# Block-0 products in one pass and other spacing in the order of steps, in a four-layer hybrid kernel

## The chip, the cores and the metric

The kernel runs on one core of a Trainium2 chip. The metric is the device time of one execution in microseconds; all times below are of that one core. TensorE multiplies matrices and writes to PSUM, ScalarE (ACT), VectorE (DVE) and GpSimd (POOL) do the elementwise work, and SyncE (SP) issues the DMAs.

## The reference

The input is 16 learned meta tokens followed by 1024 tokens, 1040 in all, with 1024 features in float32. Four layers follow each other, each as `h = h + branch(rmsnorm(h))`: sliding-window attention (layer 0), an mLSTM (layer 1), HGRN2 (layer 2), and attention again (layer 3). Most of the change lies in the mLSTM, which the text calls the second layer. It walks through blocks of 128 tokens (the first holds only the 16 meta tokens), per head with keys of 128 and values of 256:

```python
qk  = (q @ k.T) * exp(D - m_t)                    # causal weights within the block
num = w_inter * (q @ C) + qk @ v                  # from the state, and from the block
den = w_inter * (q @ n) + qk.sum(-1)
h   = num / maximum(abs(den), exp(-m_t))
C_new = w_old * C + (w_s * k).T @ v               # state for the next block
```

HGRN2 (the third layer) is also a recurrence over blocks: a state S of 128 x 128 per head is decayed, added to by `k.T @ v`, and read by the queries of the next block.

## The kernel before, in words

**Accuracy by parts.** Most products are made of reduced-precision pieces: an operand is split into a high part h and a low part l (`split`: ScalarE copies h at L196, VectorE subtracts to get l at L197), and a product is three matmuls into the same accumulator, h by h, h by l and l by h. Projections are such triples over eight pieces of 128 features (L232 with the weights stationary, L282 with the tokens stationary for values, L327 for output projections, whose results are added to x at L330). Weights come by DMA in halves of 128 x 512 and are split in the same way.

**TensorE's order is written by hand.** Every piece of TensorE work is a step `[cost, function, prefetch]`, with a cost in planned nanoseconds (a column counts 1/2.4 ns). The program runs all steps in one long list. On the other engines the instructions of the steps are put in order by a scheduler, by data, engine and priority; `hi` raises the priority of a step's instructions by a fixed offset. A step with an empty function and a cost is only a distance. `weave(a, b)` merges two lists in proportion to their costs: it takes the next step of `a` as soon as the share of `a` that has been taken isn't above the share of `b`. A part of a projection (6 matmuls of 400, 384 or 256 columns) costs 1000, 960 or 640 and can't be divided. Weights are loaded as far ahead as the steps' costs allow (`LOOKAHEAD`, 12000).

**The second layer (`layer_b`).** For each of 8 heads, `mixer` lists for nine blocks the steps s1 (q by k, a transpose of k, then the weights W and the weighted keys kw on the other engines, each split, and the split of V), s2 (the output: W by V, and from block 1 on qw by the state C), s3 (the state: kw by V; the sum is copied into C at L1063 and split) and s4 (transposes of the result). Their costs are 320, 714, 357 and 214. Between s1 of a block and its s2 stands s1 of the next block. The list without its last three steps is woven with the projections for the next head (in head 0: keys of heads 1 and 2 and values of head 1, a planned 42987 ns). Block 0 has 16 rows: its W, kw and V are filled with zeros on GpSimd and then take the same three matmuls of 128 rows as every other block, in `product`, L998.

**The third layer (`layer_c`).** For each head and region of up to two blocks, the tail is: `tail1` (transposes of the decayed keys, L1378, copied to kT at L1380), a distance `KT_LAG`, `states` (kT by V, L1388, then VectorE makes the new S, L1395), a distance `ATT_LAG`, and `tail2` for each block (attention by V at L1409, S by the queries at L1411). Tails are woven with the next region's levels, and the whole with projections.

**Attention (`layer_a`).** Keys are projected in two tiles, each in three chunks of tokens. `evac` in `qk_proj` takes a chunk out of PSUM on ScalarE: the scaled values at L576 and the squares at L577. Some thousand planned ns later `stat` sums the squares with a matmul, L616, and still later `k_split` makes h and l of the result (L509 to L512). The same `evac` serves the query tiles (t is their number, None for keys). Softmax values Sm are normalized on GpSimd at L741 before their transposes at L756.

Of the kernel before, what the change touches and what calls it, by code (L numbers as in the profile page):

```python
# [32 lines left out]

B_COLS = 96
LOOKAHEAD = 12000.0
REST_LAG, REST_STEPS = 600.0, 10
TAIL_LAG = 600.0
PRIO = 40
ROWS, TMPS, RAWS, YS = 8, 6, 2, 3
XS = 14  # L40
GAP, BURST = 200.0, 1300.0
GATE_LAG, GATE_COLS = 2000.0, 17000.0
KT_LAG, ATT_LAG = 900.0, 600.0
NORM_AT = (4000.0, 0.7), (5000.0, 0.5), (8000.0, 0.5)
Y_LAST, Y_EARLY, Y_AHEAD = 3, 8, 2500.0
T_LAG, V_LAG = 2, 4
# [68 lines left out]
def hybrid_kernel(ctx: ExitStack, tc: tile.TileContext, ins, out, layers=(0, 1, 2, 3)):  # L115
# [13 lines left out]
    def nm(x):  # L129
        ctr[0] += 1  # L130
        return f"{x}{ctr[0]}"
# [63 lines left out]
    def split(src, h, l):  # L195
        s.copy(h, src)  # L196
        v.tensor_tensor(l, src, h.bitcast(F32), op=ALU.subtract)  # L197
# [15 lines left out]
    def proj(src, evac, chunks=CHUNKS, early=None):  # L213
        st = {}

        def pre():
            st["w"] = weights(src, "m")

        groups = []
        for n, (c0, cn) in enumerate(chunks):  # L220
            grp = []
            for part in range(4):
                def fn(n=n, c0=c0, cn=cn, part=part):
                    if part == 0:
                        st[n] = psj()
                    if part == 1 and early is not None:
                        early(n, c0, cn)
                    h, l = st["w"]
                    acc = st[n]
                    for k in (2 * part, 2 * part + 1):  # L230
                        for i, (a, b) in enumerate(((h, uh), (h, ul), (l, uh))):
                            pe.matmul(acc[:, :cn], a[:, k, :], b[:, k, c0 : c0 + cn],  # L232
                                      start=(k == 0 and i == 0), stop=(k == KT - 1 and i == 2))
# [247 lines left out]
    def layer_a(i, j, first, last, fin, scale=None):  # L481
        win, wout = ins["a_win"][j], ins["a_wout"][j]
        chunks = LAST_CHUNKS if last else CHUNKS
        R = {}
# [72 lines left out]
        def qk_proj(src, gcol, work, fsplit, ch, t=None, fetched=False):  # L557
# [79 lines left out]
                d = D_K1 if fetched else D_K0 if scaled else D_K  # L637
                return [(d[0], [(8 if scaled else 4) * cn * MM, stat, None]), (d[1], [0.0, rope, None]), (d[2], turn)]

            return proj(src, evac, ch, early if fetched else None), [finish(n, *c) for n, c in enumerate(ch)]  # L640

        def tile_of(groups, events):

# [16 lines left out]
        V = {}  # L660
# [203 lines left out]
    def layer_b(i, j, fin):  # L864
        win, wout = ins["b_win"][j], ins["b_wout"][j]
        R = {}
# [114 lines left out]
        def mixer(h):  # L981
            W = {}

            def start():
                R["h", h, 0], R["h", h, 1] = row(), row()
                fetch(0)

            def fetch(b):
                c0, cn = blk(b)
                W["rw", b] = z = R["mix"].tile([P, 2, P], F32, tag="rw", name=nm("rw"), bufs=3)  # L990
                sp.dma_start(z[:, :, :cn], R["rows_d"][:, h, c0 : c0 + cn].partition_broadcast(P))

            def parts(z, cols=P, bufs=2):
                return [R["mix"].tile([P, cols], F32R, tag=z + q, name=nm(z + q), bufs=bufs) for q in "hl"]

            def product(acc, a, c, start, stop):
                for i, (x0, x1) in enumerate(((0, 0), (0, 1), (1, 0))):
                    pe.matmul(acc, a[x0], c[x1][:, :258], start=(start and i == 0), stop=(stop and i == 2))  # L998

            def s1(b):  # L1000
                mix, q, k = R["mix"], R["q", h], R["k", h]
                c0, cn = blk(b)
                cs = slice(c0, c0 + cn)
                if b + 1 < NB:
                    fetch(b + 1)
                rb, wb = (W["rw", b][:, z, :cn] for z in range(2))
                W["V", b] = parts("V", 258)
                split(R["v", h, b][:, :258], *(z[:, :258] for z in W["V", b]))
                pq = psum("pm", 2)
                pe.matmul(pq[:cn, :cn], k[:, cs], q[:, cs], start=True, stop=True)  # L1010
# [6 lines left out]
                w = mix.tile([P, P], F32, tag="W", name=nm("W"), bufs=2)  # L1017
                if b == 0:
                    g.memset(w, 0.0)
                v.tensor_tensor(w[:cn, :cn], E[:cn, :cn], pq[:cn, :cn], op=ALU.mult)  # L1020
                W["W", b] = parts("W")
                split(w, *W["W", b])
                if b:
                    qw = mix.tile([P, P], F32, tag="W", name=nm("qw"), bufs=2)
                    v.tensor_tensor(qw, q[:, cs], wb, op=ALU.mult)
                    W["qw", b] = parts("qw")
                    split(qw, *W["qw", b])
                if b < NB - 1:
                    W["kw", b] = kh, kl = parts("kw")
                    if b == 0:  # L1030
                        for z in (kh, kl):
                            g.memset(z.bitcast(F32), 0.0)
                    last = E[:cn, cn - 1 : cn]
                    s.activation(kh[:cn], pq[:cn, 128:256], AF.Identity, scale=last)
                    v.scalar_tensor_tensor(kl[:cn], pq[:cn, 128:256], last, kh[:cn].bitcast(F32),
                                           op0=ALU.mult, op1=ALU.subtract)

            def s2(b):
                mix = R["mix"]
                c0, cn = blk(b)  # L1040
                num = psum("po", 1)
                product(num[:, :258], W["W", b], W["V", b], True, b == 0)
                if b:
                    product(num[:, :258], W["qw", b], W["Cs"], False, True)
                den = small(1)
                s.activation(den[:cn], num[:cn, 256:257], AF.Abs)
                v.tensor_tensor(den[:cn], den[:cn], R["em"][:cn, b, h : h + 1], op=ALU.max)
                v.reciprocal(den[:cn], den[:cn])
                W["hn", b] = hn = mix.tile([P, 256], F32, tag="hn", name=nm("hn"), bufs=2)
                if b == 0:  # L1050
                    g.memset(hn, 0.0)
                s.activation(hn[:cn], num[:cn, :256], AF.Identity, scale=den[:cn])

            def s3(b):
                mix = R["mix"]
                c0, cn = blk(b)
                pc = psa()
                product(pc[:, :258], W["kw", b], W["V", b], True, True)
                if b == 0:
                    W["C"] = mix.tile([P, 258], F32, tag="C", name=nm("C"), bufs=1)  # L1060
                C = W["C"][:, :258]
                if b == 0:
                    v.tensor_copy(C, pc[:, :258])  # L1063
                else:
                    v.scalar_tensor_tensor(C, C, W["rw", b][:, 1, cn - 1 : cn], pc[:, :258], op0=ALU.mult, op1=ALU.add)
                W["Cs"] = parts("C", 258, 1)
                split(C, *(z[:, :258] for z in W["Cs"]))

            def s4(b):
                c0, cn = blk(b)  # L1070
                cs = slice(c0, c0 + cn)
                pt = psum("pt", 1)
                for c in range(2):
                    pe.transpose(pt[:, c * P : c * P + P], W["hn", b][:, c * P : c * P + P], ident)
                for c in range(2):
                    v.tensor_copy(R["h", h, c][:, cs], pt[:, c * P : c * P + cn])

            steps = [[0.0, start, None]]
            for b in range(NB + 2):
# [404 lines left out]
    steps = []  # L1484
# [190 lines left out]
```

## Time and profile before

| | |
|---|---|
| median of 3 runs | 2586.45 us (2584.43 to 2587.59) |
| profiled execution | 2586.18 us |
| its span, first to last instruction | 2584.4 us |
| mean granted TensorE clock | 0.996 |
| busy: TensorE, VectorE, ScalarE, GpSimd | 98%, 79%, 67%, 9% |
| stretches, us: layer 0, layer 1, hand-over, layer 2, layer 3 | 0 to 476, to 1460, to 1540, to 2095, to the end (about) |

Matmuls are pipelined, so a matmul's own duration is longer than its distance to the next; the distance is what it costs. "Wait" is time in which TensorE had no matmul under way, with the instruction that released it. In a row of the timeline the columns are start (us), duration (us), engine, line, operation, output and inputs, shapes, count, and in brackets the wait before it. In a row of stretches they are the stretch, its length, busy time (and number of instructions) of TensorE, its weight loads, VectorE, ScalarE and GpSimd, then the granted TensorE clock (1.00 is full), the share of the DMA engines, and GB/s. In rows of a line's or tile's instructions, three durations are least, median and most in ns.

### The profile page before, as it was taken

Reading aid. Unit: us, or ns where it says so; the run is one execution under the profiler, and the core shown is the slowest. Engines: PE = TensorE matmul, PEld = TensorE weight load, DVE = VectorE, ACT = ScalarE, POOL = GpSimd, SP = SyncE. Lnnn points to the kernel's source line nnn. Section 1 sums busy time; section 2 is a strip of 40 time slices with the busy share of each in tenths; the row PEclk is TensorE's granted clock in tenths of the full one; section 3 lists DMA queues with packets and bytes.
Section 4 is the critical chain, followed back from the end, with each engine's and each line's share of the span. In section 5 each row is a group of like instructions: output and inputs, shape, how many; then the busy total and the mean of one; then the engine's idle time right before and its main releaser. Section 6 shows DMA issues by size and latency. Waiting matters only on the chain.

```text
span 2584.4 us, 55470 instructions
## 1 busy us (share of the span) xinstructions
PE 2536.4 (98%) x20646; PEld 2486.1 (96%) x20646; DVE 2034.8 (79%) x5602; ACT 1740.8 (67%) x4675; POOL 244.5 (9%) x572
## 2 busy tenths in 40 slices
PE   9999999999999999999999999999999999999999
PEld 8899989989999999999999999999999998999999
DVE  7896898786767676767677788988878988887886
ACT  8766766576565656565675758877676857767772
POOL 0321231000000000000000000010000100321220
PEclk9999999999999999999999999999999999999999
DMA  5223212022232212121221111111111113212112
GB/s 157 63 66 87 59 50 70 30 53 51 49 50 49 48 51 48 52 44 50 46 52 47 61 43 34 35 34 35 35 42 37 32 51 99 58 49 79 53 42 78
DMA packets 103344, 140.27 MB, mean 54 GB/s; under 512 B 15369, under 2 KB 58514, under 8 KB 103074
## 3 DMA queue, kind: packets, MB, share of 16 engines
q1 hardware_dynamic: 103074, 136.73, 19.4%
q8 instruction: 162, 2.65, 0.4%
q14 instruction: 108, 0.88, 0.1%
HBM read 121.83 MB, written 4.27 MB: 49 GB/s over the span
## 4 chain that ended last, share of the span: by engine, by line
PE 61%; DVE 14%; ACT 10%; DMA 2%; issue 2%; SPq 0%; POOL 0%; DVEq 0%; ACTq 0%; POOLq 0%
PE pj L232 27%; PE pj L327 14%; PE pj L282 9%; PE po L998 2%; DVE wl L197 1%; ACT Sm L738 1%; DVE Sm L735 1%; PE po L774 1%; PE pt L756 1%; PE pa L998 1%; ACT X L1299 1%; ACT wh L196 1%; PE pj L278 1%; DVE x L330 1%; DVE X L1297 1%
## 5 line engine op out<-in xcount | busy, mean ns | idle before, releaser
L232 PE MATMUL pj<-uh,wh 128*128 128x384 f32 (+2 forms) x2688 | 903.8, 336 | 6.7 <-ACT uh L402 6.2
L232 PE MATMUL pj<-ul,wh 128*128 128x384 f32 (+2 forms) x2688 | 864.9, 322 | 0.3
L232 PE MATMUL pj<-uh,wl 128*128 128x384 f32 (+2 forms) x2688 | 864.4, 322 | 0.0
L232 PEld LDWEIGHTS pj<-uh,wh 128*128 128x128 f32 x2688 | 508.6, 189 | 14.6 <-ACT uh L402 6.5
L232 PEld LDWEIGHTS pj<-ul,wh 128*128 128x128 f32 x2688 | 509.2, 189 | 4.7 <-DVE ul L197 0.8
L232 PEld LDWEIGHTS pj<-uh,wl 128*128 128x128 f32 x2688 | 507.9, 189 | 0.0
L197 DVE TENSOR_TENSOR wl<-wr,wh 128x512 fp32r<-128x512 f32 (+1 forms) x338 | 234.3, 704 | 74.3 <-ACT wh L196 71.3
L196 ACT CAST wh<-wr 128x512 fp32r<-128x512 f32 (+1 forms) x338 | 203.5, 614 | 92.8 <-DMA wr<-in_b_win 32.2
L327 PE MATMUL pj<-yh,wh 128*128 128x384 f32 (+2 forms) x768 | 253.6, 330 | 9.9 <-DVE x L330 8.3
L330 DVE TENSOR_TENSOR x<-x,pj 128x384 f32<-128x384 f32 (+2 forms) x480 | 233.9, 508 | 34.0 <-PE pj L327 32.8
L327 PE MATMUL pj<-yh,wl 128*128 128x384 f32 (+2 forms) x768 | 246.3, 321 | 0.0
L327 PE MATMUL pj<-yl,wh 128*128 128x384 f32 (+2 forms) x768 | 246.3, 321 | 0.0
L282 PE MATMUL pj<-wh,uh 128*128 128x256 f32 (+1 forms) x768 | 222.6, 290 | 0.0
L282 PE MATMUL pj<-wl,uh 128*128 128x256 f32 (+1 forms) x768 | 216.2, 282 | 0.0
L282 PE MATMUL pj<-wh,ul 128*128 128x256 f32 (+1 forms) x768 | 215.9, 281 | 0.0
L738 ACT ACTIVATE Sm<-Sm,s 128x257 f32<-128x257 f32 (+2 forms) x272 | 131.1, 483 | 89.0 <-DVE s L735 86.6
L741 POOL TENSOR_TENSOR Sm<-Sm,s 128x512 f32<-128x512 f32 (+2 forms) x136 | 139.3, 1024 | 404.3 <-DVE s L740 383.5
L196 ACT CAST yh<-r 128x384 fp32r<-128x384 f32 (+2 forms) x120 | 57.0, 479 | 153.3 <-PE pj L327 137.9
L459 ACT ACTIVATE t<-t 128x384 f32<-128x384 f32 (+2 forms) x240 | 118.2, 493 | 59.9 <-DVE t L458 58.9
L327 PEld LDWEIGHTS pj<-yh,wh 128*128 128x128 f32 x768 | 144.8, 189 | 14.0 <-DVE x L330 10.4
L327 PEld LDWEIGHTS pj<-yl,wh 128*128 128x128 f32 x768 | 145.1, 189 | 0.4
L282 PEld LDWEIGHTS pj<-wh,uh 128*128 128x128 f32 x768 | 144.7, 188 | 0.6
(323 smaller groups left out, 5702.8 us busy)
## 6 DMA issues: line engine op xcount, KB each, us to landing
wr<-in_b_win SPq DMA_DIRECT2D x124, 256.0 KB, 2.9
wr<-in_a_win SPq DMA_DIRECT2D x80, 256.0 KB, 2.8
wr<-in_c_win SPq DMA_DIRECT2D x64, 256.0 KB, 2.8
wr<-in_a_wout SPq DMA_DIRECT2D x32, 256.0 KB, 2.9
rw<-rowsd SPq DMA_DIRECT2D x64, 128.0 KB, 4.3
wr<-in_b_wout SPq DMA_DIRECT2D x32, 256.0 KB, 2.9
t<-t SPq DMA_DIRECT2D x100, 48.0 KB, 1.9
cs<-in_rope SPq DMA_DIRECT2D x11, 400.0 KB, 3.3
```

The costliest lines, as they stand in the source:

```text
L196: s.copy(h, src)
L197: v.tensor_tensor(l, src, h.bitcast(F32), op=ALU.subtract)
L232: pe.matmul(acc[:, :cn], a[:, k, :], b[:, k, c0 : c0 + cn], start=(k == 0 and i == 0), stop=(k == KT - 1 and i == 2))
L278: pe.matmul(acc[:48, :nc], um[0][:, k, :], m[:, kk, :], start=(k == 0 and m is wh), stop=(k == KT - 1 and m is wl))
L282: pe.matmul(acc[:cn, :nc], a[:, k, c0 : c0 + cn], m[:, kk, :], start=(k == 0 and j == 0), stop=(k == KT - 1 and j == 2))
L327: pe.matmul(acc[:, :cn], a[:, k, mc], b, start=(k == 0 and i == 0), stop=(k == 1 and i == 2))
L330: v.tensor_tensor(x[:, m, c0 : c0 + cn], x[:, m, c0 : c0 + cn], acc[:, :cn], op=ALU.add)
L459: s.activation(a[:, :cn], a[:, :cn], AF.Exp)
L735: v.tensor_tensor_reduce(Sm[:nq, u, :nk], S[:nq, u, :nk], R["masks"][:nq, P + mo : P + mo + nk], rq, sinks[u], ALU.add, ALU.min, st[:nq, u ...
L738: s.activation(Sm[:nq, u, : nk + 1], Sm[:nq, u, : nk + 1], AF.Exp, scale=-1.0, bias=st[:nq, u : u + 1], accum_out=den[:nq, u : u + 1])
L741: g.tensor_tensor(Sm[:nq, :, :nk], Sm[:nq, :, :nk], den[:nq].rearrange("p (u c) -> p u c", c=1).to_broadcast([nq, 2, nk]), op=ALU.mult)
L998: pe.matmul(acc, a[x0], c[x1][:, :258], start=(start and i == 0), stop=(stop and i == 2))
```

## The change

For block 0 of every head of the second layer, W, kw and V become one tile each ("stacked"). It is filled with zeros, and the three parts of 16 rows stand below each other at partitions 0, 32 and 64: W and kw as h, h, l and V as h, l, h. One matmul over 128 rows then adds the three products. The tile takes one fill on GpSimd, two copies on ScalarE and one subtraction on VectorE, on 16 partitions. V's tile had no fill before, and its copy and subtraction covered 128 partitions; kw had two fills. The costs of s2(0) and s3(0) go to 119 each, from 714 and 357. In head 0 two empty steps come in: 1600 between s1(1) and s2(0), and 800 between s1(2) and s2(1). In the third layer KT_LAG goes from 900 to 1400 and ATT_LAG from 600 to 300. In the attention layers the evacuation of the key tiles (t is None) gets the raised priority.

```diff
-KT_LAG, ATT_LAG = 900.0, 600.0
+KT_LAG, ATT_LAG = 1400.0, 300.0
...
+FIRST_LAG, REST_LAG, REST_STEPS = 1600.0, 600.0, 10
...
-            return proj(src, evac, ch, early if fetched else None), [finish(n, *c) for n, c in enumerate(ch)]
+            return proj(src, evac if t is not None else lambda *a: hi(lambda: evac(*a))(), ch,
+                        early if fetched else None), [finish(n, *c) for n, c in enumerate(ch)]
...
+            def stacked(z, cols, high, low, fill):
+                st = parts(z, cols)[0]
+                g.memset(st.bitcast(F32), 0.0)
+                for o in high:
+                    fill(st[o : o + NMETA])
+                low(st[[o for o in (0, 32, 64) if o not in high][0] :][:NMETA], st[:NMETA].bitcast(F32))
+                return st
...
-                W["V", b] = parts("V", 258)
-                split(R["v", h, b][:, :258], *(z[:, :258] for z in W["V", b]))
+                V = R["v", h, b][:cn, :258]
+                if b == 0:
+                    W["V", b] = stacked("V", 258, (0, 64), lambda o, z: v.tensor_tensor(o, V, z, op=ALU.subtract),
+                                        lambda o: s.copy(o, V))
+                else:
+                    W["V", b] = parts("V", 258)
+                    split(V, *W["V", b])
...
+                if b == 0:
+                    W["W", b] = stacked("W", P, (0, 32),
+                                        lambda o, z: v.tensor_tensor(o[:, :cn], w, z[:, :cn], op=ALU.subtract),
+                                        lambda o: s.copy(o[:, :cn], w))
...
+                    if b == 0:
+                        W["kw", b] = stacked("kw", P, (0, 32), low, high)
...
-                product(num[:, :258], W["W", b], W["V", b], True, b == 0)
+                if b == 0:
+                    pe.matmul(num[:, :258], W["W", b], W["V", b], start=True, stop=True)
...
-                product(pc[:, :258], W["kw", b], W["V", b], True, True)
+                if b == 0:
+                    pe.matmul(pc[:, :258], W["kw", b], W["V", b], start=True, stop=True)
...
+                if h == 0 and b in (1, 2):
+                    steps.append([FIRST_LAG / b, lambda: None, None])
                 if 0 <= b - 1 < NB:
-                    steps.append([714, hi(lambda b=b - 1: s2(b)), None])
+                    steps.append([714 if b > 1 else 119, hi(lambda b=b - 1: s2(b)), None])
                     if b - 1 < NB - 1:
-                        steps.append([357, hi(lambda b=b - 1: s3(b)), None])
+                        steps.append([357 if b > 1 else 119, hi(lambda b=b - 1: s3(b)), None])
```

More of the change, by code (lines that the diff above doesn't have):

```diff
@@ L35 @@
 LOOKAHEAD = 12000.0
-REST_LAG, REST_STEPS = 600.0, 10
+FIRST_LAG, REST_LAG, REST_STEPS = 1600.0, 600.0, 10
 TAIL_LAG = 600.0
@@ L1016, in s1 @@
                 s.activation(E[:cn, :cn], E[:cn, :cn], AF.Exp)
-                w = mix.tile([P, P], F32, tag="W", name=nm("W"), bufs=2)
+                w = mix.tile([P, P], F32, tag="W", name=nm("W"), bufs=2)[:cn, :cn]
+                v.tensor_tensor(w, E[:cn, :cn], pq[:cn, :cn], op=ALU.mult)
                 if b == 0:
[L1019 to L1022, printed above, removed]
+                    W["W", b] = stacked("W", P, (0, 32),
+                                        lambda o, z: v.tensor_tensor(o[:, :cn], w, z[:, :cn], op=ALU.subtract),
+                                        lambda o: s.copy(o[:, :cn], w))
+                else:
+                    W["W", b] = parts("W")
+                    split(w, *W["W", b])
                 if b:
@@ L1028, in s1 @@
                 if b < NB - 1:
-                    W["kw", b] = kh, kl = parts("kw")
+                    last = E[:cn, cn - 1 : cn]
+                    kt = pq[:cn, 128:256]
+                    high = lambda o: s.activation(o, kt, AF.Identity, scale=last)
+                    low = lambda o, z: v.scalar_tensor_tensor(o, kt, last, z, op0=ALU.mult, op1=ALU.subtract)
                     if b == 0:
[L1031 to L1036, printed above, removed]
+                        W["kw", b] = stacked("kw", P, (0, 32), low, high)
+                    else:
+                        W["kw", b] = kh, kl = parts("kw")
+                        high(kh)
+                        low(kl, kh.bitcast(F32))
             def s2(b):
@@ L1041, in s2 @@
                 num = psum("po", 1)
-                product(num[:, :258], W["W", b], W["V", b], True, b == 0)
-                if b:
+                if b == 0:
+                    pe.matmul(num[:, :258], W["W", b], W["V", b], start=True, stop=True)
+                else:
+                    product(num[:, :258], W["W", b], W["V", b], True, False)
                     product(num[:, :258], W["qw", b], W["Cs"], False, True)
@@ L1057, in s3 @@
                 pc = psa()
-                product(pc[:, :258], W["kw", b], W["V", b], True, True)
+                if b == 0:
+                    pe.matmul(pc[:, :258], W["kw", b], W["V", b], start=True, stop=True)
+                else:
+                    product(pc[:, :258], W["kw", b], W["V", b], True, True)
                 if b == 0:
```

## The prediction

> **What bounds the kernel now.** I read the page first, then the list of what TensorE waited for, then the timeline around each of those waits.
>
> ```profile
> span 2584.4 us, 55470 instructions
> ...
> PE 2536.4 (98%) x20646; PEld 2486.1 (96%) x20646; DVE 2034.8 (79%) x5602; ACT 1740.8 (67%) x4675; POOL 244.5 (9%) x572
> ```
>
> TensorE is without work for only 2584.4 - 2536.4 = 48.0 us, so there are two ways to a shorter time: fewer matmuls, or fewer of these idle microseconds. The waits of TensorE by line (total, times, longest):
>
> ```profile
> PE pt L756 <- POOL Sm L741: 9.8, 9, 2.2
> PE pj L327 <- DVE x L330: 8.3, 7, 2.1
> PE pj L232 <- ACT uh L402: 6.2, 1, 6.2
> PE pa L1388 <- ACT kT L1380: 5.7, 7, 1.2
> PE pa L616 <- ACT t L577: 2.1, 1, 2.1
> ```
>
> The first three are outside the change. L1388 (states of the third layer, 5.7) and L616 (sums of squares of the second key tile in the first layer, 2.1) are inside. The rest that is inside lies in head 0 of the second layer. Timeline, with the wait in brackets:
>
> ```profile
> 550.43 0.39 PE L998 MATMUL po<-Vh,Wh 128*128 128x258 f32 x1 [2.08 <-ACT Wh L196]
> ...
> 551.60 0.39 PE L998 MATMUL po<-Vh,Wl 128*128 128x258 f32 x1 [0.66 <-DVE Wl L197]
> ...
> 552.41 0.33 DVE L1035 SCALAR_TENSOR_TENSOR kwl<-pm,E,kwh 16x128 fp32r<-16x128 f32 x1
> ...
> 553.98 0.28 PE L998 MATMUL pa<-Vh,kwh 128*128 128x258 f32 x1
> 554.10 0.28 PE L998 MATMUL pa<-Vl,kwh 128*128 128x258 f32 x1
> ...
> 554.34 0.34 PE L232 MATMUL pj<-uh,wh 128*128 128x384 f32 x1
> ...
> 555.40 0.38 PE L1010 MATMUL pm<-q,r 128*128 128x128 f32 x2
> ...
> 558.98 0.38 PE L998 MATMUL po<-Ch,qwh 128*128 128x258 f32 x1 [1.66 <-ACT Ch L196]
> ...
> 560.10 0.48 PE L998 MATMUL po<-Cl,qwh 128*128 128x258 f32 x1 [0.74 <-DVE Cl L197]
> ```
>
> At 550.43 and 551.60 step s2(0) waits for the parts of W (2.08 + 0.66 = 2.74), at 558.98 and 560.10 step s2(1) for those of the state C that s3(0) made (1.66 + 0.74 = 2.40).
>
> **The change part by part.** Everything is summed against the profiled execution: 2586.18 us, of which 2584.4 is the span and 1.8 lies around it; the median of the three runs is 0.27 above it.
>
> One scale first. The weave counts a column as 1/2.4 ns. The six 384-column matmuls from 554.34 to 555.40 are 960 ns of plan and take 1.06 us, so planned time is multiplied by 1.10.
>
> *Fewer matmuls.* A 258-column matmul takes 0.12 us of TensorE (553.98 to 554.10). In each of 8 heads s2(0) and s3(0) go from three to one: 32 x 0.12 = **-3.8 us**. TensorE is the busy engine there, so all of it is on the path.
>
> What pays for it are the operands' pieces:
>
> ```profile
> L1034 ACT ACTIVATE kwh<-pm,E x64: 354/362/378, 550.3 to 1436.6; 128x128 fp32r<-128x128 f32 x56, 16x128 fp32r<-16x128 f32 x8
> ...
> L196 ACT CAST Vh<-v x72: 391/408/423, 488.0 to 1439.7; 128x258 fp32r<-128x258 f32 x72
> ...
> L244 POOL MEMSET v<- 128x258 f32 x12 | 3.8, 317 | 66.3 <-DVE t L374 52.3 <-PE po L1409 13.9
> ...
> L1032 POOL MEMSET kwl<- 128x128 f32 x8 | 1.7, 206 | 0.0
> ```
>
> ScalarE gets a second copy of V (about 0.41 us, since its 16 partitions hold as many elements each) and of kw (0.36); W's two 16-column copies cost about what its one 128-column copy did. That is 0.8 us per head. GpSimd gets V's fill (0.32) for the one of kwl (0.21). The two stay hidden if the operands are still there when TensorE comes. Heads 1 to 6 are alike; in head 5:
>
> ```profile
> 1209.30 0.34 DVE L1035 SCALAR_TENSOR_TENSOR kwl<-pm,E,kwh 16x128 fp32r<-16x128 f32 x1
> ...
> 1211.85 0.28 PE L998 MATMUL po<-Vh,Wh 128*128 128x258 f32 x1
> ...
> 1214.60 0.28 PE L998 MATMUL pa<-Vh,kwl 128*128 128x258 f32 x1
> 1215.93 0.43 DVE L197 TENSOR_TENSOR Cl<-C,Ch 128x258 fp32r<-128x258 f32 x1
> ...
> 1217.62 0.28 PE L998 MATMUL po<-Cl,qwh 128*128 128x258 f32 x1
> ```
>
> The last operand of block 0 is ready at 1209.64, s2(0) starts at 1211.85: 2.2 us of cover for 0.8. Without cover it would be 0.8 x 7 = 5.6 us. With the new costs 119, s3(0) follows s2(0) at once, instead of after two parts of a projection; it needs the same operands, so the same cover holds. Then come two parts (1000 and 960 planned; 960 and 960 before) up to s2(1), and Cl, ready at 1216.36 for a use at 1217.62, keeps its 1.3 us. I cost both at nothing.
>
> *Head 0.* Its mixer steps sum to 12946 planned ns before and 12946 - 595 - 238 + 2400 = 14513 after, its fill to 42987 both times, so a mixer ns draws 3.32 ns of fill before and 2.96 after. Rounded up to whole parts (1000, 960, 640), the fill between s1(0) and s2(0) is 3000 before (2 x 320 x 3.32 = 2125) and 6880 after ((640 + 1600) x 2.96 = 6635). TensorE reaches s2(0) 3880 x 1.10 = 4.3 us later in its work; the lateness there was 2.74, and the added copies are 0.8: gone. kwl ended at 552.74 and would be wanted later still. Between s3(0) and s2(1) the fill goes from 1920 to 3560 (with the 800 of the second empty step): 1.8 us more against 2.40 of waiting. If C comes as late as now, 0.6 stays. Sum **-4.5 us**; with C earlier it would be -5.1.
>
> *The clock.* TensorE's granted clock (column after POOL) halves right after some of these waits:
>
> ```profile
> 242.79:246.21 3.42, 2.26 (x10) 1.59 (x10) 2.71 (x5) 2.19 (x7) 0.00 (x0) 1.00 0.37 103
> 246.21:249.62 3.41, 3.41 (x14) 3.24 (x13) 2.13 (x6) 3.21 (x9) 0.00 (x0) 0.50 0.20 62
> ...
> 556.83:560.24 3.41, 1.01 (x6) 0.60 (x5) 3.37 (x12) 3.04 (x9) 0.10 (x1) 1.00 0.00 0
> 560.24:563.65 3.41, 3.41 (x14) 3.41 (x15) 2.46 (x11) 2.81 (x9) 0.00 (x0) 0.50 0.00 0
> ...
> 546.59:550.00 3.41, 1.76 (x11) 1.43 (x10) 2.75 (x9) 2.88 (x8) 0.00 (x0) 1.00 0.06 8
> ```
>
> From 560.24 to 563.65, after a stretch in which TensorE was busy 1.01 of 3.41 us, it did half the work: 1.7 us lost. With the wait at s2(1) down to 0.6 the stretch is 80% busy: **-1.7 us**. That a stretch with 1.76 busy (the last row) had no such follower shows that the point is not sharp. The Trainium skill (TensorE: Matmul & The Clock Gate, "The HAM clock gate") gives idle windows of about 3.4 us as what halves the clock; the longest wait of this trace after the start is 2.2 us, so by that sentence these two halvings would not hang on the waits, and the sum would be 3.4 us smaller. The trace puts a halving right behind the wait, and I follow it.
>
> *Third layer.* KT_LAG adds 500 and ATT_LAG takes 300 in the chain transposes, states, output. One of the waits, and head 5's second region:
>
> ```profile
> 1652.24 0.49 PE L1388 MATMUL pa<-v,kT 128*128 128x128 f32 x2 [1.16 <-ACT kT L1380]
> ...
> 1926.15 0.61 PE L1388 MATMUL pa<-v,kT 128*128 128x128 f32 x4
> ...
> 1929.37 0.72 DVE L1395 SCALAR_TENSOR_TENSOR S<-S,s,pa 128x128 f32<-128x128 f32 x2
> ...
> 1930.13 0.39 PE L1411 MATMUL po<-X,S 128*128 128x128 f32 x2
> ```
>
> Going through the weave for all 40 regions with both settings, five of the seven waits on kT get one more projection part in front (960 to 1280 planned, 1.06 to 1.41 us against waits of 1.16 at most): region 0 of heads 1, 3 and 5, region 4 of heads 2 and 7. Head 0's first and head 6's last get none, because the parts are too coarse, and keep 1.23 and 0.93 us. That is 5.7 - 2.2 = 3.5 removed. But from states to the matmul that reads the new S, 27 of 32 distances shrink (mean over the 32: 1.24 planned us). Above, S is ready at about 1929.71 (the first of two) and read at 1930.13; the distance shrinks by 1280 x 1.10 = 1.41, so 1.0 us of waiting on S appears. Worked likewise, region 1 of heads 7 and 1 gives 0.6 and 0.2; all others have the room. Net 3.5 - 1.8 = **-1.8 us** (bounds -3.5 and +1).
>
> *Evacuation of the keys.* It now goes out with raised priority in both attention layers.
>
> ```profile
> 234.40 0.28 PE L232 MATMUL pj<-uh,wl 128*128 128x256 f32 x1
> ...
> 237.61 1.20 ACT L196 CAST wh<-wr 128x512 fp32r<-128x512 f32 x2 [4.05 <-PE pa L616]
> ...
> 243.51 0.38 ACT L577 ACTIVATE t<-pj 128x256 f32<-128x256 f32 x1
> ...
> 243.95 0.70 PE L616 MATMUL pa<-t,masks 128*128 128x256 f32 x2 [2.13 <-ACT t L577]
> ```
>
> The projection is done at 234.7 and its squares only at 243.89, behind weight casts and the splitting of the first chunk; without the wait TensorE would want them at 241.8. ScalarE is free for them from 238.8 at the latest, so ahead of that queue they are in time: -2.1, and the halved stretch 246.21 to 249.62 goes with it, -1.7: **-3.8 us**. What is pushed back is one chunk's splitting, wanted much later. Bounds: -3.8 and, if another evacuation is pushed behind it instead, +1.
>
> Sum: -3.8 - 4.5 - 1.7 - 1.8 - 3.8 = -15.6; 2586.18 - 15.6 = 2570.6, and with the 0.27 to the median **2571 us**. About 0.2% (5.2 us) is what a measurement of this kernel can tell from no change: faster is below 2581.3, slower above 2591.6.
>
> **The rivals.**
>
> *The clock goes on dropping.* The halved stretches stand on a fixed grid of 3.41 us, and shorter waits may still trip them: 3.4 us of the sum stay, 2574.3. The row at 246.21 speaks for it (the stretch before was 2.26 busy), the one at 546.59 against. This is also what the Trainium skill's page on the clock gate would give. Chance 0.12.
>
> *The raised priority does nothing for L616*, because ScalarE's queue is held by a cast that waits for TensorE (4.05 us before 237.61): 2574.7. Chance 0.10.
>
> *The waits come back elsewhere.* ScalarE and VectorE get a new order, and the kinds of wait that the change doesn't touch (35 us of the 48) may grow by what the others lose. Then only the matmuls' 3.8 us are left: 2582.6. For it speaks VectorE's 79%; against it, that no wait of TensorE in heads 1 to 7 of the second layer is listed. Chance 0.14.
>
> *S becomes the bound* (slower). The matmuls that read it, and its updates:
>
> ```profile
> L1411 PE MATMUL po<-X,S x128: 275/275/275, 1607.3 to 2085.0; 128*128 128x128 f32 x128
> L1395 DVE SCALAR_TENSOR_TENSOR S<-S,s,pa x56: 320/339/351, 1607.4 to 2081.8; 128x128 f32<-128x128 f32 x56
> ```
>
> If VectorE comes to S later, now that states run later against its other work, the shorter way from states to S's reader decides. The new distances of the 32 regions begin at 1.95, 2.35 and 2.66 us; 15 are below 4 and 17 below 5. At a latency of 5.0 us they add up to 27 us of waiting, and the time is 2570.9 - 1.8 + 27 = 2596. It is slower than 2591.6 from about 4.7 us on. S now takes 0.8 to 3.4 us after the last matmul of states (head 5 above: 3.3). Chance 0.08.
>
> **How the numbers follow.** The forecast has the remaining 0.56, between 2566 (C early, no wait on S, and one of the untouched waits falling better on the clock's grid) and 2577 (operands of block 0 uncovered, +5.6). The range is 2565 to 2582.5: it leaves out the slower rival, half of the one that keeps only the matmuls, and a few hundredths below. Faster: 0.56 + 0.12 + 0.10 and a small part of 0.14, 0.80; same 0.12; slower 0.08.
>
> **What would show it.** In the changed kernel's profile: 20614 matmuls instead of 20646, and no wait of TensorE on W in head 0; at most 0.6 us on C there, and full clock behind it; five of seven waits on kT gone, with up to 1.8 us on S at the matmul that reads it (now L1411); no wait on the key squares, and full clock around 246 us. The forecast is wrong if S or the block-0 operands head the list of waits, or if the waits on Sm and x grow by more than 5 us.

## The result and the profile after

| | before | after |
|---|---|---|
| median of the runs on one chip | 2586.55 us (8 runs, 2582.47 to 2589.45) | 2595.90 us (8 runs, 2589.10 to 2602.56) |
| ratio after to before | | 1.0036, 95% interval 1.0022 to 1.0050 |
| profiled execution (span) | 2586.18 us (2584.4) | 2602.56 us (2600.8) |

The change makes the kernel slower by 0.36%, about 9.3 us; the forecast was 15.6 us faster, and the range did not hold the result. The profiled execution of the changed kernel is the longest of its eight, 6.7 us above their median; why they differ so much comes out below, with the clock.

From the page of the changed kernel, the span and the busy times of TensorE, its weight loads, VectorE, ScalarE and GpSimd:

```profile
span 2600.8 us, 55374 instructions
...
PE 2542.7 (98%) x20614; PEld 2489.9 (96%) x20614; DVE 2036.1 (78%) x5602; ACT 1750.8 (67%) x4699; POOL 244.3 (9%) x572
```

The 32 matmuls are gone (20646 to 20614). TensorE is without work for 2600.8 - 2542.7 = 58.1 us, against 48.0: 10.1 us more waiting. What it waited for (total, times, longest), the changed kernel:

```profile
PE po L1008 <- ACT Ch L196: 11.1, 7, 2.3
PE pt L757 <- POOL Sm L742: 9.7, 9, 2.8
PE pj L327 <- DVE x L330: 8.3, 7, 2.1
PE pj L232 <- ACT uh L402: 6.7, 1, 6.7
PE po L1008 <- DVE Cl L197: 3.1, 8, 0.7
PE po L1438 <- DVE S L1422: 2.9, 4, 1.2
PE pa L1415 <- ACT kT L1407: 2.6, 2, 1.4
PE pm L728 <- DVE x L330: 2.0, 2, 1.6
PE pa L616 <- ACT t L577: 1.6, 1, 1.6
...
PE po L1436 <- DVE att L1373: 0.6, 1, 0.6
```

Sm, x and uh, which the change doesn't touch, stand within 0.5 us of where they stood. The waits on kT fell from 5.7 to 2.6, those on the key squares from 2.1 to 1.6, and waits on S came in with 2.9. At the head of the list stands the high part of the state C, 11.1 us in 7 places. Before, this wait stood in one place, in head 0:

```profile
PE po L998 <- ACT Ch L196: 1.7, 1, 1.7
```

Two of the seven are in head 0 (the longer is the first row below); the other five are one in each of heads 1 to 5 of the second layer, all at step s2(5), the output of block 5, which reads the state that s3(4) made. From the timeline of the changed kernel, TensorE's, VectorE's and SP's rows in one listing (C at L1090 is the addition of the sum pa into the state; E at L1029 is the first of VectorE's instructions of a step s1, and needs two fetched rows, rw):

```profile
563.82 0.39 PE L1008 MATMUL po<-Ch,qwh 128*128 128x258 f32 x1 [1.82 <-ACT Ch L196]
564.91 0.39 PE L1008 MATMUL po<-Cl,qwh 128*128 128x258 f32 x1 [0.71 <-DVE Cl L197]
...
726.70 0.38 PE L1008 MATMUL po<-Ch,qwh 128*128 128x258 f32 x1 [1.41 <-ACT Ch L196]
...
838.70 8.68 SPq L992 DMA_DIRECT2D rw<-rowsd  x2
...
843.01 0.35 DVE L1029 SCALAR_TENSOR_TENSOR E<-rw,bcol,caus 128x128 f32<-128x128 f32 x1 [1.59 <-DMA rw<-rowsd]
...
844.78 0.28 PE L1008 MATMUL pa<-Vh,kwl 128*128 128x258 f32 x1
...
846.50 0.48 DVE L1090 SCALAR_TENSOR_TENSOR C<-C,rw,pa 128x258 f32<-128x258 f32 x1
...
851.30 0.35 DVE L1029 SCALAR_TENSOR_TENSOR E<-rw,bcol,caus 128x128 f32<-128x128 f32 x1 [1.90 <-DMA rw<-rowsd]
...
853.97 0.28 PE L1008 MATMUL pa<-Vh,kwl 128*128 128x258 f32 x1
...
858.40 0.48 DVE L1090 SCALAR_TENSOR_TENSOR C<-C,rw,pa 128x258 f32<-128x258 f32 x1
...
859.38 0.38 PE L1008 MATMUL po<-Ch,qwh 128*128 128x258 f32 x1 [1.38 <-ACT Ch L196]
...
994.78 0.38 PE L1008 MATMUL po<-Ch,qwh 128*128 128x258 f32 x1 [2.34 <-ACT Ch L196]
...
1129.59 0.39 PE L1008 MATMUL po<-Ch,qwh 128*128 128x258 f32 x1 [1.97 <-ACT Ch L196]
...
1263.91 0.39 PE L1008 MATMUL po<-Ch,qwh 128*128 128x258 f32 x1 [1.75 <-ACT Ch L196]
```

The five add up to 1.41 + 1.38 + 2.34 + 1.97 + 1.75 = 8.85 us. The same place of head 2 in the timeline of before, with no wait at the matmul that reads Ch:

```profile
837.00 7.12 SPq L991 DMA_DIRECT2D rw<-rowsd  x2
...
842.91 0.28 PE L998 MATMUL pa<-Vh,kwl 128*128 128x258 f32 x1
...
843.23 0.48 DVE L1065 SCALAR_TENSOR_TENSOR C<-C,rw,pa 128x258 f32<-128x258 f32 x1 [0.64 <-PE pa L998]
...
848.85 0.33 DVE L1014 SCALAR_TENSOR_TENSOR E<-rw,bcol,caus 128x128 f32<-128x128 f32 x1
...
851.38 0.28 PE L998 MATMUL pa<-Vh,kwl 128*128 128x258 f32 x1
...
853.10 0.47 DVE L1065 SCALAR_TENSOR_TENSOR C<-C,rw,pa 128x258 f32<-128x258 f32 x1
...
855.28 0.28 PE L998 MATMUL po<-Ch,qwh 128*128 128x258 f32 x1
```

The bracket in the E row is the point. SP fetches the rows of a block into one of three row tiles, and the fetch for block 6 takes the tile of block 3, which is free when s3(3) has read it, that is when the first C of each listing is done. Before, that C found VectorE waiting for it (0.64) and started 843.23 - 842.91 = 0.32 us after the last matmul of its sum; now it stands behind other work of VectorE and starts 846.50 - 844.78 = 1.72 us after. Ahead of it, E of block 5 (the row at 843.01) had itself waited 1.59 us for its rows, which it had not before. SP's second issue follows: its row ends at 838.70 + 8.68 = 847.38, against 837.00 + 7.12 = 844.12. From issue to landing such a fetch takes a median of 4.3 us in both profiles. So E waits 1.90 us, where it had not waited. VectorE starts nothing else in those 1.90 us; all that stands behind E in its order waits as well. The next C starts 858.40 - 853.97 = 4.4 us after its last matmul (853.10 - 851.38 = 1.7 before), and TensorE, which comes for it in the meantime, waits 1.38.

*The clock.* Rows of stretches in the changed kernel (length, busy time and number of instructions of TensorE, weight loads, VectorE, ScalarE, GpSimd, then the granted clock, the DMA share and GB/s):

```profile
27.35:30.76 3.41, 3.12 (x25) 3.04 (x24) 0.81 (x3) 3.41 (x10) 0.00 (x0) 1.00 0.36 102
30.76:34.17 3.41, 3.41 (x7) 1.15 (x6) 1.45 (x3) 0.94 (x7) 0.00 (x0) 0.50 0.30 75
...
856.78:860.19 3.41, 1.79 (x13) 1.38 (x12) 3.41 (x10) 2.63 (x7) 0.00 (x0) 1.00 0.45 156
860.19:863.60 3.41, 3.41 (x17) 3.41 (x18) 2.38 (x11) 1.91 (x7) 0.00 (x0) 0.50 0.63 34
```

Right behind three of the five new waits TensorE runs one stretch of 3.41 us at half clock (from 860.19, 996.73 and 1129.85), 1.7 us each. Read over the whole span in such rows, this execution spent 34.1 us at half clock (ten stretches) and that of before 20.5 (six): (34.1 - 20.5) / 2 = 6.8 of the 16.4 us between the two profiled executions. The first two rows show a pair of such stretches near the start that before didn't have, behind a stretch in which TensorE was busy 3.12 of 3.41 us.

By stretch, between the same matmuls of output projections in both timelines (477.72 and 1542.57 us before, 480.70 and 1559.68 after): the first layer takes 3.0 us more, with 3.4 from the pair of slow stretches; the second layer 14.1 more; all that follows 0.7 less.

### The profile page after: what moved, and what is told of

It reads as the page before. It is cut to its first block, busy times and chain, and to the rows that moved or that the text cites. A ratio compares the mean times of both kernels' runs of the same rounds, so it can differ in the third digit from the quotient of the medians.

```text
span 2600.8 us, 55374 instructions
## 1 busy us (share of the span) xinstructions
PE 2542.7 (98%) x20614; PEld 2489.9 (96%) x20614; DVE 2036.1 (78%) x5602; ACT 1750.8 (67%) x4699; POOL 244.3 (9%) x572
## 4 chain that ended last, share of the span: by engine, by line
PE 62%; DVE 14%; ACT 8%; DMA 3%; issue 2%; SPq 0%; POOL 0%; DVEq 0%; ACTq 0%
PE pj L232 29%; PE pj L327 15%; PE pj L282 8%; DMA rw<-rowsd 2%; DVE wl L197 1%; PE po L1008 1%; DVE r L963 1%; PE po L775 1%; ACT Sm L739 1%; PE pt L757 1%; DVE q L963 1%; DVE Sm L736 1%; PE pm L1350 1%; DVE t L458 1%; ACT wh L196 1%
## 5 line engine op out<-in xcount | busy, mean ns | idle before, releaser
L330 DVE TENSOR_TENSOR x<-x,pj 128x384 f32<-128x384 f32 (+2 forms) x480 | 234.4, 509 | 34.1 <-PE pj L327 32.9
L282 PEld LDWEIGHTS pj<-wl,uh 128*128 128x128 f32 x768 | 146.8, 191 | 0.3
```

Of the source, the lines that this page charges most:

```text
L282: pe.matmul(acc[:cn, :nc], a[:, k, c0 : c0 + cn], m[:, kk, :], start=(k == 0 and j == 0), stop=(k == KT - 1 and j == 2))
L330: v.tensor_tensor(x[:, m, c0 : c0 + cn], x[:, m, c0 : c0 + cn], acc[:, :cn], op=ALU.add)
```

## The experiments

**The theory**: the new costs of s2(0) and s3(0) (119 each) in heads 1 to 7 move the later steps against the projections, and the row fetch with its three tiles turns that into a late C at block 5. **Rivals**: the stacked operands themselves are dear; the wider spacing in head 0 or in the third layer pushes the rest out of place; the raised priority of the keys delays other work. All ratios are against the kernel before on the same chip.

**Stacked products alone** (everything else as before):

```diff
-KT_LAG, ATT_LAG = 1400.0, 300.0
+KT_LAG, ATT_LAG = 900.0, 600.0
...
-                if h == 0 and b in (1, 2):
-                    steps.append([FIRST_LAG / b, lambda: None, None])
...
-                    steps.append([714 if b > 1 else 119, hi(lambda b=b - 1: s2(b)), None])
+                    steps.append([714, hi(lambda b=b - 1: s2(b)), None])
...
-                        steps.append([357 if b > 1 else 119, hi(lambda b=b - 1: s3(b)), None])
+                        steps.append([357, hi(lambda b=b - 1: s3(b)), None])
```

(and the key evacuation as before)

> Only the stacked block-0 operands with one matmul each; costs 714 and 357, spacing and priorities as in the kernel before. Theory A (the costs 119 shift block 0's successors in heads 1 to 5, so that C of block 4 comes late): no wait on Ch in heads 1 to 5 and the 32 matmuls gained, about 2583 us (2586.5 - 3.8). Theory B (the second copies of V and kw on ScalarE make C late): the waits on Ch in heads 1 to 5 are there, 2.0 to 3.0 us each, about 2595 us.

Measured: 2579.16 us, 0.9979 (0.9969 to 0.9988), 5.4 us faster by the ratio (2584.44 beside it). There is no wait on Ch in heads 1 to 5. The stacked operands are not dear.

**The new costs alone**, on the kernel before, which keeps its three matmuls:

```diff
-                    steps.append([714, hi(lambda b=b - 1: s2(b)), None])
+                    steps.append([714 if b > 1 else 119, hi(lambda b=b - 1: s2(b)), None])
...
-                        steps.append([357, hi(lambda b=b - 1: s3(b)), None])
+                        steps.append([357 if b > 1 else 119, hi(lambda b=b - 1: s3(b)), None])
```

> The kernel before with only the costs of s2(0) and s3(0) at 119 in all heads: three matmuls each as before, no empty steps. Theory A: the waits on Ch at block 5 of heads 1 to 5 appear (about 2.4 us each, 12 together) and the clock drops behind some, 2598 to 2606 us. Theory B: as before, 2586 us.

Measured: 2599.05 us, 1.0062 (1.0048 to 1.0075), 14.6 us slower by the medians. Two numbers in the source, without a single other instruction, bring the wait on the state. Waits of TensorE in this kernel; all five on Ch are at block 5 of heads 1 to 5, as in the changed kernel:

```profile
PE po L998 <- ACT Ch L196: 8.4, 5, 1.9
PE po L998 <- DVE Cl L197: 2.4, 7, 0.9
```

**The changed kernel with the old costs in heads 1 to 7**:

```diff
-                    steps.append([714 if b > 1 else 119, hi(lambda b=b - 1: s2(b)), None])
+                    steps.append([714 if b > 1 or h else 119, hi(lambda b=b - 1: s2(b)), None])
...
-                        steps.append([357 if b > 1 else 119, hi(lambda b=b - 1: s3(b)), None])
+                        steps.append([357 if b > 1 or h else 119, hi(lambda b=b - 1: s3(b)), None])
```

> The changed kernel with costs 714 and 357 for s2(0) and s3(0) in heads 1 to 7; head 0 keeps 119 and its two empty steps, the rest is as changed. Theory A: the waits of heads 1 to 5 (12 us and their clock drops, 3 x 1.7) go, 2579 to 2584 us. Theory B: they stay, about 2596 us.

Measured: 2579.20 us, 0.9977 (0.9966 to 0.9987). Against the full change (1.0036) that is 0.59%, 15 us. The wait on Ch is 2.3 us, all of it in head 0.

**The changed kernel with a fourth row tile**, which cuts the chain at the fetch and leaves TensorE's instructions in the order that the change gives them:

```diff
-                W["rw", b] = z = R["mix"].tile([P, 2, P], F32, tag="rw", name=nm("rw"), bufs=3)
+                W["rw", b] = z = R["mix"].tile([P, 2, P], F32, tag="rw", name=nm("rw"), bufs=4)
```

> The changed kernel with four row tiles (rw) in place of three, so that the rows of block 6 are fetched after C of block 2 and not after C of block 3. If VectorE's wait on those rows (1.9 us at E of block 6) is what makes C of block 4 late in heads 1 to 5, those waits shrink by about 1.9 us each and the time is 2583 to 2588 us. If C is late because of what stands ahead of it in VectorE's order, the waits stay within 0.5 us of now and the time is about 2595 us.

Measured: 2577.01 us, 0.9972 (0.9961 to 0.9983). Waits of TensorE in it:

```profile
PE po L1008 <- ACT Ch L196: 2.3, 2, 1.8
...
PE po L1008 <- DVE Cl L197: 1.4, 2, 0.7
```

Both waits on Ch are those of head 0. VectorE's waits for the rows between 680 and 1300 us (heads 1 to 5), in the changed kernel, before, and with the fourth tile:

```profile
DVE E L1029 <- DMA rw<-rowsd: 58.0, 30, 3.6
```

```profile
DVE E L1014 <- DMA rw<-rowsd: 37.7, 20, 3.4
```

```profile
DVE E L1029 <- DMA rw<-rowsd: 4.4, 5, 0.9
```

The order of steps that loses 15 us with three row tiles loses nothing with four.

One thing besides the fetch differs: in the second layer the scheduler puts some instructions of VectorE and ScalarE in another order. At the place shown above, E of block 6 now stands 12 instructions later and has no wait. The two C in this kernel:

```profile
837.93 0.47 DVE L1090 SCALAR_TENSOR_TENSOR C<-C,rw,pa 128x258 f32<-128x258 f32 x1
...
844.25 0.33 DVE L1029 SCALAR_TENSOR_TENSOR E<-rw,bcol,caus 128x128 f32<-128x128 f32 x1
...
847.88 0.47 DVE L1090 SCALAR_TENSOR_TENSOR C<-C,rw,pa 128x258 f32<-128x258 f32 x1
```

VectorE runs the same 27 instructions from one C to the next in both kernels, the other order notwithstanding. They take 847.88 - 837.93 = 9.95 us here and 858.40 - 846.50 = 11.90 in the changed kernel: the difference, 1.95, is E's wait of 1.90 and little else.

**The fourth row tile on the kernel before**:

> The kernel before with four row tiles instead of three, nothing else. If the row fetch matters only where the new costs put s3 right in front of it, VectorE's waits on the rows in the second layer become fewer than 30 us but TensorE's list keeps its waits within 1 us and the time is the same, 2584 (2581 to 2587). If the row tiles bounded the kernel before too, 4 us come off, 2580, and the gain of the four row tiles in the changed kernel would be partly a gain that has nothing to do with the change.

Measured: 2583.31 us beside 2582.68, 0.9997 (0.9987 to 1.0007). VectorE's waits on the rows fall here too, and nothing comes of it:

```profile
DVE E L1014 <- DMA rw<-rowsd: 2.6, 5, 0.6
```

So those 37.7 us were idle time of an engine with room. In these runs the wait costs only where what stands behind E makes C later than TensorE's use of it. The gain of the fourth tile in the changed kernel is the repair of the change's own damage.

**Head 0's spacing** on the stacked products alone (the two empty steps, and 119 in head 0):

```diff
+                if h == 0 and b in (1, 2):
+                    steps.append([FIRST_LAG / b, lambda: None, None])
...
-                    steps.append([714, hi(lambda b=b - 1: s2(b)), None])
+                    steps.append([714 if b > 1 or h else 119, hi(lambda b=b - 1: s2(b)), None])
...
-                        steps.append([357, hi(lambda b=b - 1: s3(b)), None])
+                        steps.append([357 if b > 1 or h else 119, hi(lambda b=b - 1: s3(b)), None])
```

> Stacked block-0 operands in all heads, and in head 0 alone the costs 119 and the two empty steps; third layer and key evacuation as in the kernel before. Stacking alone had 4.8 us of waits in head 0 and 2579.2 us. Theory of the prediction (the empty steps give the operands time): at most 0.6 us of wait on C stay, 2574 to 2575 us. Rival (VectorE has no idle time there, so that the wait only moves to C): 3.5 to 4.5 us of waits stay in head 0, 2577 to 2580 us.

Measured: 2582.91 us, 0.9993 (0.9984 to 1.0001). Head 0's waits in it and, from the same view, in the kernel without the spacing:

```profile
PE po L1007 <- ACT Ch L196: 2.3, 2, 1.8
PE po L1007 <- DVE Cl L197: 1.9, 3, 0.7
```

```profile
PE po L1062 <- ACT t L459: 3.2, 1, 3.2
...
PE po L1007 <- DVE Cl L197: 1.6, 2, 1.3
```

With spacing 2.3 + 1.9 (and 0.2 more on a product) = 4.4 us, without it 3.2 + 1.6 = 4.8: the wait on W (the row of L1062) is gone, and the waits on C have grown from 1.6 to 4.2, of which 2.5 stand at block 1 and the rest at blocks 2 and 4. That the time came out 3.7 us worse than without the spacing is more than this, and outside what both theories expected. The spacing's execution was profiled with a mean clock of 0.997 (four half-clock stretches), the other with

```profile
core 0: 2575.2 us, clock 1.000
```

It isn't only these two executions: the mean granted clock of all runs is 0.9969 with the spacing (12 runs; 0.9968 for before on that chip) and 0.9979 without (9 runs; 0.9970 for before). At 2.6 us for a thousandth of the clock, about 2 of the 3.7 us go with it (an estimate). Why it drops more often, and where the rest lies, stays open; the two intervals overlap (0.9984 to 0.9988).

**The third layer's distances** on the stacked products alone:

```diff
-KT_LAG, ATT_LAG = 900.0, 600.0
+KT_LAG, ATT_LAG = 1400.0, 300.0
```

> Stacked block-0 operands, and KT_LAG 1400 with ATT_LAG 300; all else as before. The weave worked by hand: waits on kT 6.7 to about 2.6 us, waits on S from 0 to about 2.9 us, so 2578 us against 2579.2. If the third layer had more to give: 2574 us or less.

Measured: 2578.14 us, 0.9982 (0.9972 to 0.9992): no different from 0.9979 without them. Waits in it:

```profile
PE po L1435 <- DVE S L1419: 4.7, 5, 1.5
PE pa L1412 <- ACT kT L1404: 2.6, 3, 1.2
```

4.1 us left kT (6.7 without the change of distances) and 4.7 us came on S.

**The priority of the keys** on the stacked products alone:

```diff
-            return proj(src, evac, ch, early if fetched else None), [finish(n, *c) for n, c in enumerate(ch)]
+            return proj(src, evac if t is not None else lambda *a: hi(lambda: evac(*a))(), ch,
+                        early if fetched else None), [finish(n, *c) for n, c in enumerate(ch)]
```

> Stacked block-0 operands, and raised priority for the key evacuation; all else as before. If the priority does nothing for L616 (the squares wait for their buffer, not for their turn): the wait on the key squares stays at 1.6 to 2.2 us and the time at 2579 us. If it was hidden by something else in the changed kernel: no such wait, 2575 to 2577 us.

Measured: 2576.55 us, 0.9971 (0.9961 to 0.9981), 0.08% below the kernel without it, which is inside both intervals. The wait that it was to remove stays:

```profile
PE pa L616 <- ACT t L577: 1.4, 1, 1.4
```

**The squares of that key tile in a buffer of their own**, on top of the raised priority. The squares took one of six shared tiles t, which became free only when the splitting of an earlier chunk had read it; now, in the first layer's second key tile alone, they go to tiles of another tag, of which there are three:

```diff
+        def tmps_y(n, c0, cn):
+            return [tmp()[:, :cn], tpool.tile([P, 400], F32, tag="yh", name=nm("ks"), bufs=YS)[:, :cn], tmp()[:, :cn]]
...
-        kg1, kfin1 = qk_proj(win[1], 1, tmps, k_split(1), CHUNKS, fetched=first)
+        kg1, kfin1 = qk_proj(win[1], 1, tmps_y if first else tmps, k_split(1), CHUNKS, fetched=first)
```

> As the kernel with raised priority for the key evacuation, and besides the squares of the second key tile of the first layer go into a buffer of another tag (yh), which is idle at that time, in place of one of the six shared ones. If the squares come late because their shared buffer is still being read by the splitting of the first chunk: the wait at L616 goes (1.6 to 2.2 us, and the clock drop that follows it in some executions, 1.7), 2575 to 2577 us. If they are late for ScalarE's order: the wait stays, 2579 us.

Measured: 2576.04 us, 0.9970 (0.9959 to 0.9981). The squares run at once, where they had run at 246.46 in the changed kernel and at 243.51 before, and the wait at L616 is gone from the list:

```profile
234.91 0.37 ACT L580 ACTIVATE ks<-pj 128x256 f32<-128x256 f32 x1
```

So it was the buffer that held the squares, not their priority. The rows agree: in the changed kernel and before the squares start 0.08 us after VectorE's last reading of the first chunk (L511) has ended, at 246.38 and 243.43. In time it is worth too little to tell from the kernel without it (0.5 us by the medians).

**The parts that don't harm, together**: stacked products with the old costs and no empty steps, the keys' priority and own tile, KT_LAG 1400 with ATT_LAG left at 600, four row tiles.

```diff
-KT_LAG, ATT_LAG = 900.0, 600.0
+KT_LAG, ATT_LAG = 1400.0, 600.0
...
-                W["rw", b] = z = R["mix"].tile([P, 2, P], F32, tag="rw", name=nm("rw"), bufs=3)
+                W["rw", b] = z = R["mix"].tile([P, 2, P], F32, tag="rw", name=nm("rw"), bufs=4)
```

> The stacked products with the old costs 714/357 and no empty steps, raised priority for the key evacuation with the squares of the second key tile in a buffer of their own, KT_LAG 1400 with ATT_LAG left at 600, and four row tiles. Theory: the gains are separate and add. Against the kernel with the first two (2576.0): waits on kT from about 6.7 to about 2.6 us, no wait on the new S because its distance is not cut by the smaller ATT_LAG, so 2572 (2570 to 2574). Rival: the kT waits only move to other operands of the third layer, 2576. The fourth row tile costs and brings nothing here.

Measured: 2575.83 us beside 2582.68, 0.9970 (0.9959 to 0.9982), the same as without the last two edits. The rival held: kT is gone from the list, and the wait has moved down the same tail, to S and to the squares of the output (L1447), whose sums L1453 wants, 5.0 us together where kT had 7.0 in the kernel without those two edits:

```profile
PE pa L1453 <- ACT t L1447: 3.9, 3, 1.8
...
PE po L1439 <- DVE S L1423: 1.1, 3, 0.6
```

This and the two kernels before it in the list are the fastest seen, 0.3% faster than before, with the changed kernel with four row tiles beside them (0.9972); the runs can't tell the four apart.

## Why the prediction was wrong, step by step

Parts of the change as measured, each as the difference of two ratios, times 2584:

| part | forecast | measured |
|---|---|---|
| stacked products | -3.8 | -5.4 (-8.0 to -3.1) |
| new costs, heads 1 to 7 (full change less the one with old costs there) | 0 | +15.2 |
| head 0: spacing and costs | -4.5 - 1.7 | +3.6 |
| third layer | -1.8 | +0.8 |
| priority of the keys | -3.8 | -2.1 |

They add up to +12.1, against 9.3 measured for the whole. Of the last three, head 0 is at the edge of what the runs can tell, and the other two are inside it. With the old costs in heads 1 to 7 the rest of the change gains 5.9 us (0.9977) where 15.6 were forecast, so that the other terms were too large as well.

**The step that failed is "I cost both at nothing"**, for the new costs in heads 1 to 7; they cost 15 us. The step compared planned distances from operand to use around block 0, and there it was right: no operand of block 0 in heads 1 to 7 came late. But the costs shift all later steps of a head too. I checked only the distances next to the edit, and at block 5 even the planned distance from s3(4) to s2(5) is the same with both costs, 2560. What changed was the latency on the other side: how long after the last matmul VectorE writes C, 0.3 us or 1.7 for one block, 1.7 or 4.4 for another. That latency hangs on what stands in VectorE's queue at that moment, and through the row tiles on a fetch of 4.3 us whose start was C itself. My reason against the rival "waits come back elsewhere" was that no wait in heads 1 to 7 was listed. A list of waits shows what is late, and not what is nearly late: before, at block 5 of heads 1 to 5, the copy Ch was done only 1.0 us before TensorE read it. That rival was also priced as if waits could only eat the gain; it had no price for a new chain.

**Head 0** failed at "if C comes as late as now". With more projection between its steps VectorE had more of that projection's work in front of C, and C of block 0 started 4.1 us after its matmul, against 3.2 before. ScalarE added more: its copy Ch started 2.06 us after C was written, against 0.75. Of 5.14 us of waits 4.4 stayed where I had 0.6. "Full clock behind it" held in the changed kernel's profile, where no half-clock stretch follows, but by luck: the wait at C was not shorter, and with four row tiles and the same 1.8 us of wait there a half-clock stretch does follow, from 561.95.

**The keys** failed at "ahead of that queue they are in time". The row at 237.61 showed a queue on ScalarE, and I took that for the reason; what held the instruction was the tile it writes to. In the changed kernel the squares ran even later than before, at 246.46, a wait of 1.6 us stayed, and half clock followed it again, from 249.2. The rival that the priority does nothing for L616 was right for the wrong reason: it blamed a cast that waits for TensorE.

**The third layer** was right in direction: kT to 2.6 (forecast 2.2 left), S 2.9 (1.8), and 0.6 on the attention operand. Together 2.6 + 2.9 + 0.6 - 5.7 = 0.4 us more waiting, where 1.8 less was forecast; it is inside the bounds that were given. The forecast's own terms, 3.5 and 1.8, leave 1.7 and not 1.8.

**The matmuls** were right in size: 32 fewer, and the added copies on ScalarE hidden (1740.8 to 1750.8 us busy, 1.25 a head where I had 0.8). The 5.4 us that this part brought agrees with 3.8 within its interval. Part of the 5.4 may be the clock: with what the mean granted clock cost each run taken out, 3.6 are left (an estimate, from (1 - clock) times the span of each run).

**The clock** is where the forecast argued from one pair of rows. "Right behind the wait" isn't a rule. The stretch of 1.79 us busy before 860.19 was followed by half clock, and the one of 3.12 before 30.76 as well. A wait of 3.20 us in the stacked kernel was followed by none, while waits of 3.63 and 3.67 us at the same matmul were, in the kernels with the third layer's distances and with the parts together.

What fits all twelve traces is how far the columns of TensorE's matmuls fill a stretch of the 3.41 us grid. This is an estimate: the columns of the matmuls that start in the stretch, at the plan's 1/2.4 ns each. Of the stretches at full clock, all 23 that were filled to less than 0.29 were followed by half clock, and none that was filled to more than 0.41; in between both occur. The stretch before 30.76 is busy, but filled to only 0.33, since 16 of its 25 matmuls have two columns. The grid cuts the wait of 3.20 us into two stretches, filled to 0.34 and 0.51. The grid falls differently in each trace, so one and the same wait can be followed by half clock or not. That the fill is what decides isn't shown by an experiment.

The Trainium skill (TensorE: Matmul & The Clock Gate, "The HAM clock gate") says that the clock halves after at least one idle window of about 3.4 us, on a window that runs free of the kernel. The length of 3.41 us and the fixed grid agree with it; that the window has to be idle does not, as the rows show.

How many half-clock stretches an execution has is not a property of the kernel alone: the mean granted clock of the changed kernel's eight runs goes from 0.999 in the shortest (2589.10 us) to 0.993 in the longest (2602.56), which is the one that was profiled, with ten such stretches of 1.7 us each. Six thousandths of the span are about 16 us (an estimate), enough for the 13.5 us between the two.

## What to carry to other kernels

When a change alters planned costs in a hand-written order, check every consumer downstream, and against the latency that the engines' queues give it now, not only the planned distance next to the edit. An engine that takes its instructions in order holds everything behind one that waits for a transfer: look for the transfer whose start depends on the late result itself, and count its tiles before spacing steps apart. An instruction that runs late on an idle engine may be held by the tile that it writes; raising its priority does nothing for that.

## What the runs showed of the hardware

The granted clock can halve behind a stretch in which TensorE was 91% busy (27.35 to 30.76), and stay full behind a wait of 3.20 us. In the twelve traces it always halved behind a stretch of its 3.41 us grid that matmul columns filled to less than 0.29, and never behind one filled to more than 0.41. A fetch of 128 KB takes 4.3 us from issue to landing (the median). And 20 waits of VectorE on that fetch, 37.7 us within 620, cost nothing that the runs can tell before, while 30, 58.0 us in all, go with 15 us of time.
